# Low halves of the weights: from a VectorE subtraction to a ScalarE negation and an accumulating DMA, with five raw buffers

## The chip, the core and the metric

One core of a Trainium2 chip runs the whole program in one launch. The metric is the device time of one execution in microseconds (us). The engines are TensorE (PE, with its weight loads listed apart as PEld), VectorE (DVE), ScalarE (ACT), GpSimd (POOL) and SyncE (SP), which only issues transfers here.

## What is computed

Two layers of an encoder over 512 tokens of width 1024, all in float32. Each layer has a modulated norm, one input projection into three token mixers (a convolution module, windowed attention, a two-way recurrence), an output projection, a second modulated norm and a gated feed-forward block with a width-3 convolution. The modulation vectors come from the conditioning vector `c` through `w_ada`.

```python
for l in range(DEPTH):                                   # DEPTH = 2
    mod = cond @ w_ada[l] + b_ada[l]                     # 6 x 1024 values per layer
    sh1, sc1, g1, sh2, sc2, g2 = jnp.split(mod, N_MOD, axis=-1)
    h = _rmsnorm(x, norm1_w[l]) * (1.0 + sc1) + sh1
    x = x + g1 * _token_mixers(h, w_in[l], ..., w_out[l])  # 1024 -> 3584 -> mixers -> 1024
    h = _rmsnorm(x, norm2_w[l]) * (1.0 + sc2) + sh2
    x = x + g2 * _conv_ffn(h, w_up[l], conv_f_w[l], w_down[l])   # 1024 -> 2 x 2816 -> 1024
return _rmsnorm(x, final_norm_w)
```

## The kernel before

Activations lie with channels on the 128 partitions and the 512 tokens along the free dimension. A matrix product in near-float32 precision is made from three products of `fp32r` halves: a weight `w` is split into `hi`, the value rounded to `fp32r`, and `lo = w - hi`; an activation likewise. `block` issues, for each 128x128 block of weights, `hi*hi`, `hi*lo` and `lo*hi` into the same PSUM tile.

The weights come as a list of chunks, in the order in which they are used: 128x1024 floats (512 KB) for a column of `w_in` or `w_up`, 128x512 for `w_out1`, 128x640 or 128x512 for `w_down1`, 128x768 for the first group of each stage. Three threads of the program carry them:

- `loader` (L351) takes a free raw buffer `wr` (three of them) and has SP load the next chunk into it.
- `splitter` (L358) takes a loaded chunk at most three ahead of the one in use (five for a "wide" chunk, which may also use idle buffers of other tags). It writes `hi` into a buffer `wh` on ACT or DVE, whichever the planner expects to be done first (`copy`, L396), then `lo` into a buffer `wl` on DVE (L368), and gives the raw buffer back. There are four `wh` and four `wl`.
- `next_chunks` (L372) and `tile_gemm` (L712) use them: one tile of 128 output channels at a time, 24 matmuls for a chunk of 8 blocks, 15 for one of 5, 12 for one of 4.

All program order is fixed beforehand. `Clock` books an estimated end for each instruction, and `run_threads` always advances the thread of highest priority whose needs are met by that clock. Every engine, and SP's list of loads, then runs its instructions strictly in the order so written; an instruction that waits holds all behind it on its engine.

Three more threads matter here. `ada_thread` (L524) loads the rows of `w_ada`, 512 KB at a time, into buffers named `bias` and `wa` (three in the feed-forward stage), and has DVE reduce each with one 128x1024 instruction (`ada_tile`). Most of this work for layer 1 is put into the feed-forward stage of layer 0. `ffn_col` (L1304) takes an up-projection tile out of PSUM: one ACT and two DVE operations for the convolution, a GELU on ACT for the gate, a multiplication on DVE, and a split into halves `m` (copy and subtraction). `down` (L1295) runs the down-projection of a group of five or four columns once all its `m` are there; it is placed behind the first column of the next group.

The order of a layer is: mixers (`w_in` tiles with the mixers' small products between them, then `w_out`), then the feed-forward stage (a first group of six tiles, then up tiles and `down` groups by turns, then a last group that also feeds the next norm).

Of the kernel before, what the change touches and what calls it, by code (L numbers as in the profile page):

```python
# [9 lines left out]
F32 = mybir.dt.float32  # L10
F32R = mybir.dt.float32r
U8 = mybir.dt.uint8
AF = mybir.ActivationFunctionType
ALU = mybir.AluOpType
# [6 lines left out]
KD = D // 128  # L21
# [17 lines left out]
H2 = T // 2  # L39


BUFFERS = dict(wr=(4, 3), wh=(4, 4), wl=(4, 4), hx=(4, 8), qk=(4, 2), PT=(4, 4), KK=(4, 1), QQ=(4, 1), S=(4, 1),
               TT=(6, 1), ao=(2, 2), vr=(2, 2), va=(2, 1), bias=(4, 2), wa=(4, 1), tmp=(2, 5), P=(2, 2), sc=(1, 1),
               ap=(4.25, 1), acc=(2, 2), sm=(0.03125, 8), km=(2, 1), gs=(2, 3), qr=(2, 2), t2=(2, 2))
ORDER = ["wh", "wl", "wa", "bias", "wr", "tmp", "km", "P", "ap", "acc", "gs", "qr", "vr", "va", "ao", "t2", "sc",
# [16 lines left out]
def size(ap):  # L62
    n = 1
    for d in ap.shape[1:]:
        n *= d
    return n


def span(ap):
    lo = hi = ap.offset  # L70
    for s, n in ap.ap[1:]:
        if s > 0:
            hi += s * (n - 1)
        else:
            lo += s * (n - 1)
    return lo, hi
# [21 lines left out]
DM = 1.0  # L98
# [94 lines left out]
class Kernel:  # L193
    def __init__(self, ctx, tc, a):
# [13 lines left out]
        self.free_slots, self.slot, self.count = {}, {}, 0  # L208
        for tag, (kb, n) in BUFFERS.items():
            self.free_slots[tag] = [dict(tag=tag, name=f"{tag}{i}", size=int(kb * 256), pool=self.one, last=0.0)  # L210
# [51 lines left out]
    def dma(self, out, in_, eng=None):  # L262
# [7 lines left out]
            c.w.setdefault(out.tensor.name, []).append((lo, hi, t + (4.5 if eng is self.nc.gpsimd else 2.4), "DMA"))  # L270
        c.last[sb.tensor.name] = t + 2.0

    def mm(self, out, lhsT, rhs, start, stop, **kw):
        self.nc.tensor.matmul(out, lhsT=lhsT, rhs=rhs, start=start, stop=stop, **kw)  # L274
        n, m = size(out), out.shape[0]
        c = 0.009 + n * 0.000408 if rhs.dtype == F32R else n * 0.00168 * {32: 0.5, 64: 0.51}.get(m, 1.0)
        self.clk.issue("PE", c, [out], [lhsT, rhs])
# [80 lines left out]
    def splitter(self):  # L358
        for i in range(len(self.chunks)):
            more = MTAG + ["bias", "wa", "ap"] if i in self.wide else []  # L360
            yield (lambda: 0.0 if i in self.raw and i <= self.cur_chunk + (WA if i in self.wide else 3) else None,)
            t = self.raw.pop(i)
            yield (t, [["wh"] + more, 1], [["wl"] + more, 1])
            hi = self.sb([128, 1024], ["wh"] + more, F32R)[:, :t.shape[1]]
            self.copy(hi, t)
            yield (hi, DM, [["wl"] + more, 1])
            lo = self.sb([128, 1024], ["wl"] + more, F32R)[:, :t.shape[1]]
            self.v.tensor_tensor(out=lo, in0=t, in1=hi.bitcast(F32), op=ALU.subtract)  # L368
            self.give(t)
            self.wt[i] = (hi, lo)  # L370

# [671 lines left out]
    def rec(self, l, p):  # L1043
# [13 lines left out]
        def scores(lhs, rhs, w):  # L1057

            ps = self.pst("m2", [128, 2, 512])
            for c in range(4):  # L1060
                for hd in range(2):
                    for j in range(4):
                        mm(ps[32 * j:32 * j + 32, hd, c * w:(c + 1) * w], lhs(hd, c * 128 + 32 * j),
                           rhs(hd, c * 128 + 32 * j), True, True, tile_position=(64 * hd, 32 * j))
            return ps[:, :, :4 * w].rearrange("p h (c w) -> p h c w", c=4)
# [75 lines left out]
        for d in range(2):  # L1141
            cs = range(3) if d == 0 else range(1, 4)
            kt = kts[d]
            yield (kt, "m")
            u = self.pst("m", [128, 4, 128])
            for c in cs:
                mm(u[:, c], kt[:, c], V[:, c], True, True)
            self.give(kt)
            yield (u,)
            st = self.st[d]  # L1150
            seq = list(cs) if d == 0 else list(cs)[::-1]
            for i, c in enumerate(seq):
                for hd in range(2):
                    r = slice(64 * hd, 64 * hd + 64)
                    if i == 0:
                        v.tensor_copy(st[r, i, r], u[r, c, r])
                    else:
                        v.scalar_tensor_tensor(st[r, i, r], st[r, i - 1, r], TT[r, d, 128 * c:128 * c + 1], u[r, c, r],
                                               ALU.mult, ALU.add)
            self.give(u)  # L1160
# [3 lines left out]
        for c in range(4):  # L1164
            for hd in range(2):
                mm(o[:, c, 64 * hd:64 * hd + 64], S[:, hd, c], V[:, c, 64 * hd:64 * hd + 64],
                   c == 0 and hd == 0, False)
            last = [x for x in ((1, c - 1) if c > 0 else None, (0, 2 - c) if c < 3 else None) if x]
            for i, (qi, si) in enumerate(last):
                mm(o[:, c], QQ[:, qi, c * 128:(c + 1) * 128], self.st[1 - qi][:, si],  # L1170
                   False, c == 3 and i == len(last) - 1)
# [265 lines left out]
```

## Time and profile before

| | |
|---|---|
| median of three runs | 1370.12 us (1370.08 to 1370.56) |
| the profiled execution | 1370.76 us, span 1369.0 us |
| mean granted TensorE clock | 0.991 |
| PE busy | 1344.9 us (98%) |
| DVE busy | 1070.0 us (78%) |
| ACT busy | 609.6 us (45%) |
| POOL busy | 2.1 us |
| transfers | 169.19 MB, 37.9% of the 16 DMA engines' time on SP's queue |

By the tiles that the rows name, the mixers of layer 0 run until about 317 us of the span, the feed-forward stage of layer 0 from there to about 705 us, the mixers of layer 1 to about 972 us, and its feed-forward stage to the end. A "window" row gives, for a stretch of the span, its length, each engine's busy time with the number of instructions, the granted clock, the mean busy share of the DMA engines and the rate of transfer. A "group" row gives instructions of one kind and shape: count, busy time, mean ns of one, and the idle time before them with what ended it.

### The profile page before, as it was taken

The page shows a single profiled execution, that of the slowest core. Times are in us where ns is not written, and L with a number is a line of the kernel's source. Part 1 is how long each engine was busy: PE and PEld are TensorE (multiplying, and loading weights), DVE is VectorE, ACT ScalarE, POOL GpSimd, SP SyncE. Part 2 cuts the span into 40 slices and gives each one's busy share as a digit, 9 for nine tenths or more (in the row PEclk, how much of TensorE's full clock was granted, in tenths as well). Part 3 has the DMA queues.
Part 4 walks back from the last instruction along what each step waited for, and adds up shares of the span by engine and source line. Part 5 has one row for each costly group of instructions (what it writes and reads, how often), then busy time and mean ns, then how long its engine had stood idle before and what let it go on. Part 6 is the DMA issues. An engine that isn't in the chain of part 4 may idle for free.

```text
span 1369.0 us, 24502 instructions
## 1 busy us (share of the span) xinstructions
PE 1344.9 (98%) x10042; PEld 1112.4 (81%) x10042; DVE 1070.0 (78%) x1841; ACT 609.6 (45%) x1017; POOL 2.1 (0%) x16
## 2 busy tenths in 40 slices
PE   8999999999999999999999999999999999999997
PEld 7977767778988888888899777777898888888887
DVE  6799999898599999766695999888868565556666
ACT  4537556565342433333453473746535232233332
POOL 0000000000000000000000000000000000000000
PEclk8999999999999999999999999999999999999998
DMA  9534443232348788432431312011422323323221
GB/s 353 189 134 142 124 151 94 81 105 89 103 148 293 254 280 290 126 108 70 140 99 63 106 54 99 32 53 54 139 78 57 128 76 95 101 86 122 77 93 63
DMA packets 55264, 169.19 MB, mean 124 GB/s; under 512 B 6256, under 2 KB 8304, under 8 KB 55152
## 3 DMA queue, kind: packets, MB, share of 16 engines
q1 hardware_dynamic: 55152, 167.63, 37.9%
q8 instruction: 79, 1.29, 0.4%
q14 instruction: 33, 0.27, 0.1%
HBM read 165.50 MB, written 2.10 MB: 122 GB/s over the span
## 4 chain that ended last, share of the span: by engine, by line
PE 84%; DVE 12%; ACT 2%; issue 1%; DMA 0%; SPq 0%; DVEq 0%; ACTq 0%
PE m L274 53%; PE g L274 29%; DVE acc L181 2%; PE m L280 2%; DVE KK L181 2%; DVE QQ L181 1%; DVE wl L181 1%; DVE TT L181 1%; DVE wa L181 1%; DVE P L181 1%; DVE hx L181 1%; DVE x L181 1%; DVE st L181 0%; DVE sc L181 0%; DMA x<-xT 0%
## 5 line engine op out<-in xcount | busy, mean ns | idle before, releaser
L274 PE MATMUL g<-hx,wh 128*128 128x512 f32 (+1 forms) x1288 | 402.6, 390 | 0.9 <-DVE qk L181 0.8
L274 PE MATMUL m<-hx,wh 128*128 128x512 f32 (+1 forms) x1136 | 318.0, 364 | 0.0
L181 DVE TENSOR_TENSOR wl<-wr,wh 128x1024 fp32r<-128x1024 f32 (+3 forms) x215 | 220.5, 1027 | 90.4 <-ACT wh L181 79.4
L274 PEld LDWEIGHTS g<-hx,wh 128*128 128x128 f32 x1288 | 237.2, 189 | 53.2 <-issue 7.7
L181 ACT CAST wh<-wr 128x1024 fp32r<-128x1024 f32 (+3 forms) x176 | 157.1, 893 | 250.9 <-PE m L274 155.0
L274 PE MATMUL g<-hx,wl 128*128 128x512 f32 (+1 forms) x648 | 252.7, 390 | 0.0
L274 PEld LDWEIGHTS m<-hx,wh 128*128 128x128 f32 x1136 | 204.3, 189 | 34.2 <-issue 0.6
L274 PE MATMUL m<-hx,wl 128*128 128x512 f32 (+1 forms) x576 | 209.0, 363 | 0.0
L274 PEld LDWEIGHTS g<-hx,wl 128*128 128x128 f32 x648 | 122.5, 189 | 25.4 <-issue 3.8
L274 PEld LDWEIGHTS m<-hx,wl 128*128 128x128 f32 x576 | 108.7, 189 | 16.9
L181 DVE SCALAR_TENSOR_TENSOR x<-m,mod,x 128x256 f32<-128x256 f32 (+1 forms) x112 | 66.2, 592 | 43.1 <-PE m L274 42.1
L181 DVE SCALAR_TENSOR_TENSOR acc<-ap,par,acc 128x512 f32<-128x512 f32 x120 | 89.8, 748 | 2.2
L181 DVE SCALAR_TENSOR_TENSOR tmp<-m,par,tmp 128x511 f32<-128x511 f32 x120 | 89.1, 746 | 1.9
L181 ACT ACTIVATE P<-P,sm 128x512 f32<-128x512 f32 x72 | 51.5, 721 | 42.6 <-DVE sm L181 42.2
L181 ACT ACT_TABLE_LOAD x49 | 62.9, 1283 | 6.0 <-DVE sm L181 4.5
L181 DVE CAST wh<-wr 128x1024 fp32r<-128x1024 f32 (+3 forms) x41 | 24.5, 598 | 52.4 <-PE m L274 37.1
L181 ACT ACTIVATE tmp<-tmp 128x512 f32<-128x512 f32 x44 | 27.8, 632 | 73.1 <-DVE tmp L181 73.0
L181 ACT COPY km<-KK 128x512 f32<-128x512 f32 x30 | 20.5, 683 | 80.2 <-DVE KK L181 58.8
L181 ACT ACTIVATE tmp<-m,par 128x512 f32<-128x512 f32 x60 | 40.7, 686 | 34.5 <-PE m L274 32.8
L181 DVE CUSTOM_DVE_ANT_0 bias<-bias,cb,par 128x1024 f32<-128x1024 f32 x39 | 49.5, 1278 | 2.3 <-DMA bias<-w_ada 2.3
L181 DVE CUSTOM_DVE_ANT_0 wa<-wa,cb,par 128x1024 f32<-128x1024 f32 x39 | 49.9, 1278 | 0.7 <-DMA wa<-w_ada 0.7
L181 ACT ACTIVATE tmp<-x 128x256 f32<-128x256 f32 (+1 forms) x64 | 28.4, 444 | 46.4 <-DVE x L181 42.4
(319 smaller groups left out, 2158.0 us busy)
## 6 DMA issues: line engine op xcount, KB each, us to landing
wr<-w_up SPq DMA_DIRECT2D x76, 512.0 KB, 3.5
wr<-w_in SPq DMA_DIRECT2D x44, 512.0 KB, 3.5
bias<-w_ada SPq DMA_DIRECT2D x39, 512.0 KB, 4.5
wa<-w_ada SPq DMA_DIRECT2D x39, 512.0 KB, 4.0
wr<-w_down SPq DMA_DIRECT2D x32, 320.0 KB, 2.9
wr<-w_down SPq DMA_DIRECT2D x32, 256.0 KB, 2.6
wr<-w_in SPq DMA_DIRECT2D x16, 384.0 KB, 4.4
wr<-w_up SPq DMA_DIRECT2D x16, 384.0 KB, 3.3
```

The source lines that it names most:

```text
L181: r = f(*a, **k)
L274: self.nc.tensor.matmul(out, lhsT=lhsT, rhs=rhs, start=start, stop=stop, **kw)
L280: self.nc.tensor.transpose(out, in_, self.ident)
```

## The change

For every chunk but the first eight of layer 0 (`i < KD`), the subtraction on DVE is taken out. ACT writes `-hi` into the `wl` buffer, and a DMA that GpSimd issues then adds the raw chunk to it in place (`accum_op=ALU.add`, from `wr` to `wl`, both on chip). The raw buffer is free once that transfer has landed, and the `lo*hi` matmul waits for it. The planner books such an add on a line of its own, beside that of the loads. There are five raw buffers in place of three; the room comes from a smaller scratch area for GpSimd's descriptors.

```diff
-BUFFERS = dict(wr=(4, 3), wh=(4, 4), wl=(4, 4), ...
+BUFFERS = dict(wr=(4, 5), wh=(4, 4), wl=(4, 4), ...
...
+    def add_dma(self, out, in_):
+        self.nc.gpsimd.dma_start(out=out.bitcast(F32), in_=in_, accum_op=ALU.add)
+        c = self.clk
+        t = max(c.t.get("ADD", 0.0), c.t["PE"], c.written(out) or 0.0) + size(in_) * in_.shape[0] * 4 / 200e3
+        c.t["ADD"] = t
+        lo, hi = span(out)
+        l = c.w.setdefault(out.tensor.name, [])
+        l[:] = [e for e in l if not (lo <= e[0] and e[1] <= hi)] + [(lo, hi, t + 2.4, "DMA")]
+        c.last[in_.tensor.name] = c.last[out.tensor.name] = t + 2.4
...
             hi = self.sb([128, 1024], ["wh"] + more, F32R)[:, :t.shape[1]]
             self.copy(hi, t)
-            yield (hi, DM, [["wl"] + more, 1])
             lo = self.sb([128, 1024], ["wl"] + more, F32R)[:, :t.shape[1]]
-            self.v.tensor_tensor(out=lo, in0=t, in1=hi.bitcast(F32), op=ALU.subtract)
+            yield (hi, DM) if i < KD else (hi,)
+            if i < KD:
+                self.v.tensor_tensor(out=lo, in0=t, in1=hi.bitcast(F32), op=ALU.subtract)
+            else:
+                self.s.activation(lo, hi.bitcast(F32), AF.Copy, scale=-1.0)
+                yield (lo,)
+                self.add_dma(lo, t)
             self.give(t)
...
-    nc = bacc.Bacc("TRN2", target_bir_lowering=False, num_devices=1)
+    nc = bacc.Bacc("TRN2", target_bir_lowering=False, num_devices=1, dynamic_dma_scratch_size=4096)
```

Counted in the written order, 240 chunks change: 136 of 128x1024, 48 of 128x512, 32 of 128x640 and 24 of 128x768, 103.8 MB in all. Since the planner's clock for DVE changes, the whole order is written anew. Two places show what that does.

The first is SP's list of loads in the feed-forward stage of layer 0, before and then with the change. `wr<-w_down` is a chunk of weights; `wa<-w_ada` and `bias<-w_ada` are rows of the modulation matrix of layer 1.

```order
L263 DMA wr_781_5136<-w_down 128x640
L263 DMA bias_782_5144<-w_ada 128x1024
L263 DMA wr_788_5173<-w_down 128x640
L263 DMA wa_789_5185<-w_ada 128x1024
L263 DMA bias_793_5199<-w_ada 128x1024
L263 DMA wr_795_5217<-w_down 128x640
L263 DMA bias_796_5226<-w_ada 128x1024
L263 DMA wr_802_5252<-w_down 128x640
L263 DMA wa_803_5266<-w_ada 128x1024
L263 DMA bias_804_5274<-w_ada 128x1024
```

Here one or two modulation loads stand between two chunks of weights.

```order
L263 DMA wr_780_5170<-w_down 128x640
L263 DMA wa_781_5173<-w_ada 128x1024
L263 DMA bias_782_5183<-w_ada 128x1024
L263 DMA bias_783_5193<-w_ada 128x1024
L263 DMA wr_788_5212<-w_down 128x640
L263 DMA wa_789_5221<-w_ada 128x1024
L263 DMA bias_791_5234<-w_ada 128x1024
L263 DMA bias_796_5255<-w_ada 128x1024
L263 DMA wr_797_5264<-w_down 128x640
L263 DMA wa_798_5276<-w_ada 128x1024
```

With the change three stand there. The second place is DVE in the same stretch. `ISA` with a `wa` or `bias` operand is the reduction of one modulation load, `SCALAR_TENSOR_TENSOR tmp` the two convolution steps of an up tile, `TENSOR_TENSOR wl` the subtraction for `lo`.

```order
L181 TENSOR_TENSOR wl_801_5242<-wr_781_5136,wh_798_5234 128x640
L181 SCALAR_TENSOR_TENSOR tmp_800_5238<-m_0_791_5193,par,tmp_800_5238 128x511 x2
L181 TENSOR_TENSOR PT_797_5230<-tmp_792_5195,PT_797_5230 128x512
L181 ISA wa_789_5185,mod_157<-wa_789_5185,cb,par 128x1024
L181 ISA mod_157 128x1
L181 ISA bias_793_5199,mod_157<-bias_793_5199,cb,par 128x1024
L181 ISA mod_157 128x1
L181 TENSOR_TENSOR wl_808_5286<-wr_788_5173,wh_805_5278 128x640
L181 SCALAR_TENSOR_TENSOR tmp_807_5282<-m_799_5236,par,tmp_807_5282 128x511 x2
```

Between the convolution steps of two tiles DVE has a subtraction and two reductions.

```order
L181 SCALAR_TENSOR_TENSOR tmp_795_5245<-m_786_5198,par,tmp_795_5245 128x511 x2
L181 ISA wa_789_5221,mod_159<-wa_789_5221,cb,par 128x1024
L181 ISA mod_159 128x1
L181 SCALAR_TENSOR_TENSOR amul_161<-mod_159,par 128x1
L181 ISA bias_791_5234,mod_159<-bias_791_5234,cb,par 128x1024
L181 ISA mod_159 128x1
L181 ISA bias_796_5255,mod_159<-bias_796_5255,cb,par 128x1024
L181 ISA mod_159 128x1
L181 SCALAR_TENSOR_TENSOR amul_161<-mod_159,par 128x1
L181 SCALAR_TENSOR_TENSOR tmp_803_5293<-m_794_5243,par,tmp_803_5293 128x511 x2
```

With the change the subtraction is gone and a third reduction stands in its place. On ACT each `CAST wh` is now followed, one or two instructions later, by an `ACTIVATE wl<-wh` of the same width. TensorE's order has the same instructions, with the mixers' small products placed anew among the `w_in` tiles.

More of the change, by code (lines that the diff above doesn't have):

```diff
@@ L39 @@
 H2 = T // 2
-BUFFERS = dict(wr=(4, 3), wh=(4, 4), wl=(4, 4), hx=(4, 8), qk=(4, 2), PT=(4, 4), KK=(4, 1), QQ=(4, 1), S=(4, 1),
+BUFFERS = dict(wr=(4, 5), wh=(4, 4), wl=(4, 4), hx=(4, 8), qk=(4, 2), PT=(4, 4), KK=(4, 1), QQ=(4, 1), S=(4, 1),
                TT=(6, 1), ao=(2, 2), vr=(2, 2), va=(2, 1), bias=(4, 2), wa=(4, 1), tmp=(2, 5), P=(2, 2), sc=(1, 1),
```

## The prediction

> **What bounds the kernel now.** I read the page's busy shares first, then windows by stage, then the groups of the instructions that change, then the transfers.
>
> ```profile
> PE 1344.9 (98%) x10042; PEld 1112.4 (81%) x10042; DVE 1070.0 (78%) x1841; ACT 609.6 (45%) x1017; POOL 2.1 (0%) x16
> ```
>
> The page gives shares over the whole span; the windows say where PE is not full. Columns: stretch, its length, PE, PEld, DVE, ACT, POOL busy, granted clock, DMA share, GB/s.
>
> ```profile
> 15.00:65.00 50.00, 49.06 (x450) 44.92 (x450) 40.77 (x91) 22.67 (x48) 0.18 (x2) 0.91 0.76 270
> 65.00:120.00 55.00, 54.09 (x743) 42.09 (x742) 53.66 (x92) 25.71 (x45) 0.00 (x0) 1.00 0.46 152
> 120.00:180.00 60.00, 58.13 (x530) 42.28 (x528) 54.96 (x105) 36.46 (x60) 0.00 (x0) 1.00 0.38 115
> 180.00:250.00 70.00, 69.73 (x716) 51.47 (x716) 63.29 (x128) 43.32 (x83) 0.00 (x0) 0.98 0.40 128
> 250.00:317.00 67.00, 62.52 (x669) 43.84 (x669) 57.89 (x118) 41.90 (x77) 0.00 (x0) 1.00 0.27 83
> 375.00:668.00 293.00, 293.00 (x1294) 242.34 (x1293) 244.02 (x359) 101.50 (x143) 0.00 (x0) 1.00 0.57 188
> 740.00:820.00 80.00, 80.00 (x872) 61.77 (x872) 76.04 (x146) 47.31 (x80) 0.00 (x0) 1.00 0.22 72
> 820.00:900.00 80.00, 79.81 (x862) 59.70 (x859) 71.11 (x130) 42.98 (x77) 0.00 (x0) 1.00 0.18 59
> 900.00:972.00 72.00, 70.74 (x824) 52.78 (x823) 60.35 (x124) 45.12 (x85) 0.00 (x0) 1.00 0.30 89
> ```
>
> PE bounds nearly all of it. In the feed-forward stretch (375 to 668) it is busy for every microsecond: 293.00 us over 1294 matmuls are 0.2264 us each, so an up tile of 24 takes 5.43 us, a chunk of five blocks 3.40, one of four 2.72. In the mixers DVE is 90 to 98% busy, but PE idles only 0.91 + 1.87 + 0.27 + 4.48 = 7.5 us in layer 0 and 0.19 + 1.26 = 1.5 us in layer 1. Freeing DVE can win at most these 9.0 us, since the matmuls themselves stay.
>
> **The change, part by part.** Groups: busy, mean ns | idle before.
>
> ```profile
> L181 DVE TENSOR_TENSOR wl<-wr,wh 128x1024 fp32r<-128x1024 f32 x123 | 150.2, 1222 | 74.4 <-ACT wh L181 64.6 <-PE m L274 6.0 <-PE m L280 0.3
> L181 DVE TENSOR_TENSOR wl<-wr,wh 128x512 fp32r<-128x512 f32 x48 | 32.9, 686 | 8.9 <-ACT wh L181 8.0
> L181 DVE TENSOR_TENSOR wl<-wr,wh 128x640 fp32r<-128x640 f32 x32 | 26.1, 819 | 6.5 <-ACT wh L181 6.2
> L181 DVE TENSOR_TENSOR wl<-wr,wh 128x768 fp32r<-128x768 f32 x12 | 11.4, 952 | 0.7 <-ACT wh L181 0.6
> L181 ACT CAST wh<-wr 128x1024 fp32r<-128x1024 f32 x100 | 105.0, 1050 | 146.6 <-PE m L274 96.1 <-PE g L274 36.6 <-DMA wr<-w_up 9.2
> L181 ACT CAST wh<-wr 128x512 fp32r<-128x512 f32 x38 | 23.6, 621 | 42.6 <-PE g L274 21.3 <-PE m L274 21.1
> ```
>
> *Subtractions off DVE.* 136 x 1.222 + 48 x 0.686 + 32 x 0.819 + 24 x 0.952 = 248 us of DVE go. DVE is on PE's path only in the mixers; of the 9.0 us I take 2 as won, since 22 subtractions of 1.22 us in each layer's `w_in` tiles are some 27 us of about 230, an eighth of DVE's load, and part of the idle time is released by ACT. Ends: 0 and -9.
>
> *Negations on ACT.* A pass of the same width over on-chip data is nearest to the CAST rows: 1.05 us for 1024, 0.62 for 512. 240 of them make about 216 us, and ACT rises from 45% to some 60%. Taken at nothing: in the feed-forward stretch ACT is busy 101.5 of 293 us. If that cover went, `hi` of later chunks would be late, which the chain below prices.
>
> *Five raw buffers.* At the start two more chunks of 384 KB are loaded ahead of the modulation rows, with the DMA engines full. That is 0.79 MB at about 410 GB/s, 1.9 us; PE idles 0.94 us of 50 there, so little absorbs it, but these rows also have slack in their buffers. I take +1, ends 0 and +2. Elsewhere SP has more lead, which costs nothing.
>
> *The adds.* No row shows a transfer from GpSimd or between on-chip buffers. Two things must be priced: how late one lands, and how much of the DMA engines it takes. First the lateness, bounded by loads (size, us from issue to landing):
>
> ```profile
> wr<-w_up SPq DMA_DIRECT2D x76, 512.0 KB, 3.5
> wr<-w_down SPq DMA_DIRECT2D x32, 256.0 KB, 2.6
> PT<-w_sh SPq DMA_DIRECT2D x5, 512.0 KB, 8.2
> ```
>
> The chain for a chunk becomes cast, negation, add. Three chunks are split ahead: 16.3 us for up tiles, 8.2 us for four-block chunks. At the quiet end it takes 2 x 0.62 + 2.6 = 3.8 us for 256 KB and 2 x 1.05 + 3.5 = 5.6 for 512 KB; with the 8.2 us of a load into full queues, 9.4 and 10.3. I take the quiet end, since outside the start and the burst below the queues are less than half busy: covered, at nothing.
>
> Now the load on the DMA engines. This is the stretch that decides, the burst of modulation loads in layer 0's feed-forward stage, beside the start of the program, where the engines run full:
>
> ```profile
> 10.00:15.00 5.00, 4.81 (x27) 4.71 (x28) 2.09 (x4) 2.95 (x5) 0.00 (x0) 0.50 1.03 417
> 20.00:25.00 5.00, 5.00 (x41) 4.39 (x40) 4.86 (x10) 1.70 (x5) 0.00 (x0) 0.64 1.04 408
> 411.00:445.00 34.00, 34.00 (x151) 27.91 (x150) 30.97 (x49) 9.93 (x12) 0.00 (x0) 1.00 0.83 292
> 445.00:479.00 34.00, 34.00 (x152) 28.15 (x151) 32.72 (x50) 13.84 (x20) 0.00 (x0) 1.00 0.78 254
> 479.00:513.00 34.00, 34.00 (x152) 28.15 (x151) 33.29 (x55) 10.05 (x15) 0.00 (x0) 1.00 0.82 280
> 513.00:548.00 35.00, 35.00 (x156) 29.00 (x155) 33.08 (x49) 12.36 (x17) 0.00 (x0) 1.00 0.83 287
> ```
>
> The same stretch, DVE's reductions and what DVE waited for (us in total, times, longest):
>
> ```profile
> L181 DVE CUSTOM_DVE_ANT_0 bias<-bias,cb,par 128x1024 f32<-128x1024 f32 x31 | 39.4, 1278 | 2.3 <-DMA bias<-w_ada 2.3
> L181 DVE CUSTOM_DVE_ANT_0 wa<-wa,cb,par 128x1024 f32<-128x1024 f32 x16 | 20.4, 1278 | 0.5 <-DMA wa<-w_ada 0.5
> DVE bias L181 <- DMA bias<-w_ada: 2.3, 2, 1.4
> DVE wa L181 <- DMA wa<-w_ada: 0.5, 1, 0.5
> ```
>
> Before, DVE paces the burst (33 of 34 us busy) and the DMA engines are 80% busy, so DVE loses only 2.8 us to late loads. With the subtraction gone the written order fills DVE with reductions. Laying PE's order out at 0.2264 us a matmul, the 102 us from the first `down` on hold 45 modulation loads where they held 32. That is 45 x 0.524 = 23.6 MB, and the weights bring 65.5 KB per 0.679 us, 9.8 MB: 33.4 MB, 328 GB/s, before a single add. The adds carry another 9.8 MB.
>
> At the 410 GB/s of the full engines the loads take 81.5 us and the adds 23.9 us times a factor k. A load reads a byte once and writes it once. An add reads two operands and writes one, so k lies between 1 and 2, and I take 1.5 by that count of passes. Together that is 105, 117 or 129 us for k = 1, 1.5, 2 against 102 us of PE work: late by 3, 15 or 27 us. At the poorer rate of the burst itself (0.83 busy at 290, so 350 GB/s when full) and k = 2 it is 151 us, late by 49.
>
> Late loads hold DVE, which is in order, and behind the reductions stand the convolution steps. What lies between them and PE:
>
> ```profile
> L181 ACT ACTIVATE tmp<-m,par 128x512 f32<-128x512 f32 x60 | 40.7, 686 | 34.5 <-PE m L274 32.8 <-DVE KK L181 1.1 <-DVE tmp L181 0.6
> L181 DVE SCALAR_TENSOR_TENSOR tmp<-m,par,tmp 128x511 f32<-128x511 f32 x120 | 89.1, 746 | 1.9
> L181 DVE TENSOR_TENSOR tmp<-tmp,tmp 128x512 f32<-128x512 f32 x48 | 32.9, 689 | 4.5 <-ACT tmp L181 3.6
> L181 ACT CAST PT<-tmp 128x512 fp32r<-128x512 f32 x16 | 9.9, 620 | 42.7 <-DVE tmp L181 42.7
> L181 DVE TENSOR_TENSOR PT<-tmp,PT 128x512 fp32r<-128x512 f32 x16 | 11.0, 691 | 8.2 <-ACT PT L181 8.2
> ```
>
> A group's last column needs 0.69 + 2 x 0.75 + 0.69 + 0.62 + 0.69 = 4.2 us after its tile, and `down` starts two up tiles, 10.9 us, later: 6.7 us of slack. ACT's GELU waits for the same DVE steps, and the casts and negations stand behind it. So PE loses the lateness less 6.7 us: 8 us for k = 1.5, none for k = 1, 20 for k = 2, 42 at the worst end.
>
> A rule of the Trainium skill speaks against that cost. "DMA: Bandwidth & Descriptors", section "Anatomy of one DMA — SWDGE (gpsimd) path", fits a transfer from GpSimd as about 2.0 us plus its bytes at 436 GB/s; by it the adds would weigh like copies, the burst would hold, and the sum would end at the second rival below. No run here shows it for an add.
>
> **The sum:** -2 + 0 + 1 + 0 + 8 = +7 us on the profiled execution's 1370.76 us (0.6 us above the median of the runs): 1377 after rounding down the tenths.
>
> **The rivals.**
>
> *Adds too slow one by one* (slower). With the landing of the 8.2 us row the chain for 256 KB is 9.4 us, above the lead of 8.2 us, the point from which it decides. With four `wl` buffers a chunk then takes a quarter of chain plus use. At 12 us that is (12 + 2.72) / 4 = 3.68 us for 2.72, and 48 chunks of that width lose 46 us: about 1416. For it: nothing shows how fast GpSimd issues. Against it: a chain above 8.2 us needs a landing three times the quiet one. The Trainium skill's "SBUF — State Buffer", section "Who interferes with whom", says that DVE copies and casts in a two-port mode lock GpSimd out while they run, and descriptors wait; it adds to this chance, and no run here shows it.
>
> *Adds like copies* (faster). With k = 1 the burst is late by 3 us, less than the slack; the start costs nothing, and the mixers keep 3 to 9 of their idle us: 1361 to 1367, say 1365. For it: DVE's 90 to 98% in the mixers. Against it: the burst has 3 us of margin over a fully loaded DMA.
>
> *Nothing to win* (same). The burst holds, and the new order of the mixers' small products idles PE as much as the old one: 1369 to 1372.
>
> **How the numbers follow.** A difference of 0.2%, 2.7 us, is about what a measurement of this kernel can tell from none. The crowded burst has 0.46 (0.43 slower, 0.03 within), slow adds 0.14 (slower), adds like copies 0.25 (0.22 faster, 0.03 within), nothing to win 0.15 (0.09 within, 0.03 on either side). Faster 0.25, same 0.15, slower 0.60. The likeliest case is 1377, its own range 1373 (the slack eats most) to 1410 (350 GB/s, k = 2). The range takes in adds like copies but for its best end and the crowded burst but for its worst: 1363 to 1406.
>
> **What would show it.** In the burst, DVE's waits for `bias` and `wa` loads rise from 2.8 us to over 15, the DMA share goes to about 1.0, and PE is no longer busy for all of the stretch. Over the span DVE falls to about 840 us and ACT rises to about 800; PE's idle time in the mixers stays within 9 us. If the burst's waits stay at a few us, the price of an add (k) was too high; if PE waits for DMA into `wl`, the add's landing was underestimated. A time above 1410 or below 1361 makes the prediction wrong altogether.

## The result, and the profile after

| | before | with the change |
|---|---|---|
| median | 1370.15 us (1370.08 to 1370.56) | 1444.35 us (1440.78 to 1446.29) |
| the profiled execution | 1370.76 us, span 1369.0 us | 1440.78 us, span 1439.0 us |
| mean granted clock | 0.991 | 0.980 |

The medians are of four runs each (for before, the three of the table ahead and one of 1370.19 us). The ratio is 1.0538 (interval 1.0515 to 1.0561): the change costs 74 us. The prediction had the sign (slower, 1377 us) and a tenth of the size; 1444 us lies above its range and above the 1410 us that it called wrong altogether.

The page's first part, to be held against the row of before:

```profile
PE 1364.9 (95%) x10042; PEld 1126.1 (78%) x10042; DVE 874.8 (61%) x1648; ACT 771.4 (54%) x1205; POOL 210.9 (15%) x256
```

DVE lost the work it was to lose (195 us less: the 240 subtractions are gone, and some casts and copies came over from ACT) and ACT took the negations (162 us more: those into `wl` alone are 191, and 19 casts of weights moved to DVE). TensorE does the same 10,042 matmuls, yet idles 74 us of its span where it idled 24. The other 20 us of the 70 are in its busy time, 1364.9 us against 1344.9, at a lower mean clock (0.980 against 0.991). What is new is in the third part: queue, packets, MB, and the time of those packets as a share of 16 engines' span.

```profile
q0 software_dynamic: 34560, 103.82, 39.5%
q1 hardware_dynamic: 55152, 167.63, 34.1%
```

The adds (q0) carry 62% as many bytes as the loads and occupy the DMA engines longer. 103.82 MB in 0.395 x 1439.0 = 568 us are 183 GB/s; the loads run at 167.63 MB in 491 us, 342 GB/s. An added byte costs 1.87 loaded ones, or 2.24 at the 410 GB/s of full engines that the prediction used.

And in the sixth part: size, median us from issue to landing.

```profile
wl<-wr POOLq DMA_DIRECT2D x122, 512.0 KB, 6.2
wl<-wr POOLq DMA_DIRECT2D x48, 256.0 KB, 3.8
wr<-w_up SPq DMA_DIRECT2D x76, 512.0 KB, 5.8
bias<-w_ada SPq DMA_DIRECT2D x39, 512.0 KB, 7.7
```

An add of 512 KB lands 6.2 us after its issue where the prediction took 3.5, and the loads beside it became slower too (`w_up` 5.8 from 3.5, `bias` 7.7 from 4.5).

**Where the time went.** Both traces hold the same matmuls, and at the borders of stages in the same order. So the start of the n-th matmul in one trace less its start in the other tells how much had been lost by then, and differences of these give each stage its share. (Inside the mixers the small products stand in another order, so there only two kernels with the same order can be compared.) In us against the profiled execution of before, stages named by before's times; the experiments in the columns on the right follow below. The traced executions of the change, the copy and the spread are the shortest of their kernels, 4 to 8 us under the medians.

| stage | the change | no add | copy, not add | wide on DVE | spread | both |
|---|---|---|---|---|---|---|
| mixers of layer 0 with their last group, to 340 | +11.0 | -8.0 | -7.5 | +2.5 | +13.6 | +7.2 |
| the burst, 340 to 560 | +28.0 | -0.2 | +8.2 | +32.3 | +2.9 | +3.0 |
| rest of the up tiles, 560 to 668 | +0.2 | 0.0 | +0.6 | +5.0 | +2.3 | +2.5 |
| last group of that stage, to 736 | +11.5 | 0.0 | +2.8 | 0.0 | +12.8 | 0.0 |
| mixers of layer 1, to 971 | +4.3 | +4.0 | +4.0 | +4.0 | +4.1 | +4.8 |
| their last group, to 996 | +6.2 | 0.0 | 0.0 | 0.0 | +5.2 | 0.0 |
| feed-forward of layer 1, to 1324 | +0.2 | 0.0 | 0.0 | +2.0 | +1.1 | +1.6 |
| its last group and the end | +8.8 | +0.1 | +1.4 | 0.0 | +8.0 | +0.5 |
| total | +70.2 | -4.1 | +9.5 | +45.7 | +50.0 | +19.6 |

Two places carry most of the 70: the burst (28) and the last groups (11.5 + 6.2 + 8.8, and of the first row the 8.5 that go when the wide chunks stay on DVE, together 35).

**The burst.** The windows that the prediction showed of before, now with the change (length, PE, PEld, DVE, ACT, POOL busy, granted clock, DMA share, GB/s):

```profile
411.00:445.00 34.00, 34.00 (x151) 28.00 (x150) 22.07 (x38) 15.72 (x21) 6.03 (x7) 1.00 1.02 294
445.00:479.00 34.00, 28.76 (x125) 22.81 (x123) 19.75 (x34) 10.89 (x14) 4.34 (x5) 1.00 1.04 337
479.00:513.00 34.00, 28.85 (x108) 23.11 (x109) 25.11 (x41) 14.95 (x22) 4.30 (x5) 0.85 1.02 306
513.00:548.00 35.00, 28.86 (x112) 22.69 (x111) 25.91 (x46) 14.46 (x21) 6.89 (x8) 0.90 1.03 320
440.00:560.00 120.00, 102.73 (x412) 81.60 (x412) 78.38 (x134) 46.36 (x60) 17.28 (x20) 0.93 1.03 321
```

The DMA engines are full throughout, DVE is no longer busy, and from the second row on PE runs 108 to 125 matmuls where it ran 152 to 156. In the 120 us of the last row PE idles 17.3 us. Its 412 matmuls are 93.3 us of work at the 0.2264 us of before and took 102.7, so the lower clock (0.93) cost another 9.4 us. The waits of that stretch that bear on it (us in total, times, longest):

```profile
POOL wl L275 <- ACT wl L181: 97.0, 19, 10.5
ACT wh L181 <- DMA wr<-w_up: 25.1, 7, 5.3
DVE bias L181 <- DMA bias<-w_ada: 25.0, 15, 3.2
DVE wa L181 <- DMA wa<-w_ada: 18.4, 9, 2.8
ACT PT L181 <- DVE tmp L181: 18.0, 3, 8.2
ACT tmp L181 <- DVE tmp L181: 16.0, 5, 8.2
...
PE m L285 <- DMA wl<-wr: 11.0, 4, 5.2
PE g L285 <- DMA wl<-wr: 3.5, 2, 2.0
```

DVE waits for the modulation rows (43 us), and ACT for the convolution steps that stand behind them on DVE, up to 8.2 us at a time. Before, from 411 to 548 us, the longest such wait was 3.3 us:

```profile
ACT tmp L181 <- DVE tmp L181: 16.7, 7, 3.3
```

PE waits in the end for `wl`, the add. What made the add late is seen in the way to the longest of these waits (start, us, what, and in brackets the idle time before and its releaser):

```profile
463.68 1.29 DVE L181 CUSTOM_DVE_ANT_0 bias<-bias,cb,par 128x1024 f32<-128x1024 f32 x1 [1.31 <-DMA bias<-w_ada]
...
467.45 1.29 DVE L181 CUSTOM_DVE_ANT_0 bias<-bias,cb,par 128x1024 f32<-128x1024 f32 x1 [2.48 <-DMA bias<-w_ada]
...
468.86 1.52 DVE L181 SCALAR_TENSOR_TENSOR tmp<-m,par,tmp 128x511 f32<-128x511 f32 x2
470.48 0.63 ACT L181 ACTIVATE tmp<-tmp 128x512 f32<-128x512 f32 x1 [8.23 <-DVE tmp L181]
471.01 1.03 ACT L181 CAST wh<-wr 128x1024 fp32r<-128x1024 f32 x1
...
473.88 0.87 POOL L275 DMA_DIRECT2D wl<-wr  x1 [10.45 <-ACT wl L181]
...
482.11 0.79 PE L285 MATMUL m<-hx,wl 128*128 128x512 f32 x1 [5.21 <-DMA wl<-wr]
```

Two reductions wait for their rows, the convolution steps come late, ACT's GELU waits 8.2 us for them, and the cast and the negation of a chunk of weights stand behind the GELU. The add, issued at 473.9, needs 8.2 us to land, and PE stands still for 5.2 us. The waits of 2.0 and 3.5 us at 503 and 531 us came the same way, behind ACT's waits of 8.2 and 5.9 us for DVE; with the first they are 10.7 of the 14.5 us that PE waits for `wl`. The shorter waits at 448 and 455 us (3.2 together) follow casts that waited 3.5 and 4.1 us for late loads of weights. Over the 20 adds of the stretch the landing took 5.6 to 9.8 us, median 8.6.

**The last groups.** At the end of a stage several wide chunks are wanted at once, and their `lo` lies in idle buffers of other tags. Of the transfers issued from 130 to 330 us, which ends with the last group of layer 0's mixers:

```profile
wl<-wr POOLq DMA_DIRECT2D x11, 512.0 KB, 5.9
...
TT<-wr POOLq DMA_DIRECT2D x1, 512.0 KB, 9.4
S<-wr POOLq DMA_DIRECT2D x1, 512.0 KB, 10.8
qk<-wr POOLq DMA_DIRECT2D x1, 512.0 KB, 12.8
```

The adds into `TT`, `S` and `qk` were issued within 3 us of each other and landed one after another, after 9.4, 10.8 and 12.8 us. The end of layer 1's feed-forward stage shows what PE makes of it (start, us, and in brackets the idle time before and its releaser):

```profile
1399.14 0.39 PE L285 MATMUL m<-PT,ap 128*128 128x256 f32 x1 [1.87 <-DMA ap<-wr]
1399.37 0.39 PE L285 MATMUL m<-KK,S 128*128 128x256 f32 x2
1401.62 0.39 PE L285 MATMUL m<-KK,QQ 128*128 128x256 f32 x1 [1.86 <-DMA QQ<-wr]
1401.84 0.56 PE L285 MATMUL m<-TT,wh 128*128 128x256 f32 x2
1404.10 0.58 PE L285 MATMUL m<-TT,wl 128*128 128x256 f32 x1 [1.70 <-DMA wl<-wr]
```

### The profile page after: what moved, and what is told of

It is laid out like the page before. It is cut to its first block, busy times and chain, and to the rows that moved or that the text cites. A ratio compares the mean times of both kernels' runs of the same rounds, so it can differ in the third digit from the quotient of the medians.

```text
span 1439.0 us, 25211 instructions
## 1 busy us (share of the span) xinstructions
PE 1364.9 (95%) x10042; PEld 1126.1 (78%) x10042; DVE 874.8 (61%) x1648; ACT 771.4 (54%) x1205; POOL 210.9 (15%) x256
## 3 DMA queue, kind: packets, MB, share of 16 engines
q0 software_dynamic: 34560, 103.82, 39.5%
q1 hardware_dynamic: 55152, 167.63, 34.1%
## 4 chain that ended last, share of the span: by engine, by line
PE 64%; DMA 14%; issue 10%; DVE 8%; ACT 2%; POOL 1%; SPq 0%; POOLq 0%; DVEq 0%; ACTq 0%
PE m L285 39%; PE g L285 23%; DMA wl<-wr 3%; DMA bias<-w_ada 2%; DMA wa<-w_ada 2%; DMA qk<-wr 2%; DMA wr<-w_up 2%; DVE acc L181 1%; PE m L291 1%; DMA wr<-w_down 1%; DMA wa<-w_sh 1%; DVE st L181 1%; POOL wl L275 1%; DVE wa L181 1%; DVE tmp L181 1%
## 5 line engine op out<-in xcount | busy, mean ns | idle before, releaser
L285 PE MATMUL g<-hx,wh 128*128 128x512 f32 (+1 forms) x1304 | 408.7, 391 | 1.3 <-ACT tmp L181 1.3
L275 POOL DMA_DIRECT2D wl<-wr x213 | 185.1, 869 | 1125.1 <-ACT wl L181 958.0
L285 PE MATMUL m<-hx,wh 128*128 128x512 f32 (+1 forms) x1104 | 312.9, 368 | 0.0
L181 ACT CAST wh<-wr 128x1024 fp32r<-128x1024 f32 (+3 forms) x157 | 137.6, 876 | 171.0 <-PE m L285 73.4
L285 PEld LDWEIGHTS m<-hx,wh 128*128 128x128 f32 x1104 | 200.3, 190 | 34.0 <-issue 0.4
L285 PE MATMUL m<-hx,wl 128*128 128x512 f32 (+1 forms) x560 | 206.0, 368 | 8.7 <-DMA wl<-wr 8.7
L181 ACT ACTIVATE wl<-wh 128x1024 fp32r<-128x1024 f32 (+3 forms) x212 | 190.7, 900 | 43.0 <-DVE wh L181 39.1
L181 DVE CAST wh<-wr 128x1024 fp32r<-128x1024 f32 (+3 forms) x60 | 37.4, 623 | 141.2 <-PE m L285 113.6
L181 DVE SCALAR_TENSOR_TENSOR tmp<-g,par,tmp 128x511 f32<-128x511 f32 x56 | 41.8, 749 | 22.9 <-ACT tmp L181 21.9
```

The costliest lines, as they stand in the source:

```text
L181: r = f(*a, **k)
L275: self.nc.gpsimd.dma_start(out=out.bitcast(F32), in_=in_, accum_op=ALU.add)
```

## The experiments

The theory to be tested: an add is a dear transfer (about twice a load's time on the DMA engines, 6 us and more to land), and it costs at two places for two reasons, the burst by throughput and the last groups by latency. The rivals: that the change's other parts cost (five raw buffers, the negations on ACT, the new order), and that any transfer at that place, cheap or dear, would do the same. Each ratio below is against runs of before that were taken beside that kernel (medians 1370.7 to 1371.7 us).

**The wide chunks back on DVE.** The wide chunks (`self.wide`, at the ends and beginnings of the stages, 40 of the adds) are subtracted on DVE as before.

```diff
-            yield (hi, DM) if i < KD else (hi,)
-            if i < KD:
+            yield (hi, DM) if i < KD or i in self.wide else (hi,)
+            if i < KD or i in self.wide:
```

> Edit: the wide chunks (first and last groups of each stage) keep the subtraction on VectorE; all other chunks keep negation and add. Theory A (the last groups lose because their four 512 KB chunks are wanted almost at once and an add lands 6 to 12 us after issue, where the subtraction took 1.2 us): the 33 us lost at the four last groups go, the burst's 28 us stay, about 1411 us. Theory B (the adds lose only by filling the DMA engines): the last groups are not in the burst, so little changes, 1435 to 1444 us.

Measured: 1416.69 us (1410.86 to 1417.42), ratio 1.032 (1.0299 to 1.0341). In the table the last groups go to 0, and the burst stays (32.3). So the last groups' loss is the adds of their own chunks, in the first row too (8.5 us less).

**The modulation loads spread.** A distance of 5 us of TensorE's planned time between two reductions of `ada_thread` in the feed-forward stage.

```diff
-ADAG = 0.0
+ADAG = 5.0
```

> Edit: layer 1's modulation tiles are spaced at least 5 us apart by the planner (ADAG 0 to 5), so the loads of the feed-forward stage of layer 0 fall from 328 to about 200 GB/s. Theory A (burst: loads plus adds want more than the DMA engines give): the 28 us lost between the first and the second down-projection of layer 0 go, the last groups' loss stays, about 1416 us. Theory B (each add is late by itself, whatever the traffic): PE's waits for wl in that stretch stay, 1435 us or more.

Measured: 1425.22 us (1420.57 to 1426.82), ratio 1.0386 (1.0365 to 1.0406), 9 us above what was expected. The same stretch of the burst:

```profile
440.00:560.00 120.00, 117.91 (x517) 96.64 (x516) 66.45 (x106) 58.85 (x74) 22.41 (x26) 1.00 1.03 295
```

PE is busy for 117.9 of 120 us at full clock where it was busy for 102.7 at 0.93, and the loss falls from 28.0 to 2.9 us. The DMA engines still read 1.03, with fewer bytes a second: the modulation rows come later, and what is left still fills them. A share of 1 alone thus does not say that anything is late. What the stretch gained was partly given back: 2.6 us in the first row of the table, 2.1 from 560 to 668, 1.3 in the next last group.

**Both together.** The two edits above.

> Edits of the first two experiments together: wide chunks subtract on VectorE, modulation tiles spaced by 5 us. If burst and last groups are separate losses they add: about 33 and 24 us of the 70 go, and what stays is the mixers (3 to 8 us in layer 0, 4 in layer 1): 1380 to 1385 us. If one feeds the other, so that curing one cures part of the other, the sum would fall short: 1395 us or more.

Measured: 1389.54 us (1385.85 to 1391.99), ratio 1.0137 (1.0121 to 1.0153), a little above what was expected. The gains add, nearly: the last groups are at 0 as with the wide chunks alone, the burst at 3 as with the spread alone. What is left is 7.2 us in the mixers of layer 0 (4.7 more than with the wide chunks alone), 4.8 in those of layer 1, and 7.6 in small pieces of the feed-forward stages.

**A copy in place of the add.** The transfer goes between the same buffers but only copies; the low half then holds the raw weight, so this kernel computes something else.

```diff
-        self.nc.gpsimd.dma_start(out=out.bitcast(F32), in_=in_, accum_op=ALU.add)
+        self.nc.gpsimd.dma_start(out=out.bitcast(F32), in_=in_)
```

> Edit: the transfer that GpSimd issues copies the raw chunk over the buffer in place of adding to it (so the low half holds the raw weight); order, issue and bytes stay. If accumulating is what costs the DMA engines (two reads for one write), their time for the 103.8 MB falls from 39.5% of the span to about 22%, the burst's loss falls from 28 us to under 10, and the time to about 1410 us. If a transfer from GpSimd between on-chip buffers costs the same with and without the addition, the share and the time stay within 1% of 1444 us.

Measured: 1388.45 us (1380.3 to 1390.97), ratio 1.0113 (1.008 to 1.0146). Its queue, and its landings:

```profile
q0 software_dynamic: 27904, 103.82, 19.2%
```

```profile
wl<-wr POOLq DMA_DIRECT2D x122, 512.0 KB, 3.8
```

The same bytes at 103.82 MB / (0.192 x 1378.5 us) = 392 GB/s, 2.1 times the add's rate, and landed in 3.8 us where the add takes 6.2. With the same order of instructions as in the change, 56 of the 74 us go, and the time is 22 us below the 1410 us expected: the last groups gained too, which the expectation left out. So it is the accumulation, not a transfer at that place, that makes most of the loss. (The copies also went in fewer packets, 27,904 against 34,560; the next run holds the packets.) The burst still loses 8.2 us.

**Half an add.** Only the first half of each chunk's columns is added; the other half stays `-hi`.

```diff
-        self.nc.gpsimd.dma_start(out=out.bitcast(F32), in_=in_, accum_op=ALU.add)
+        n = size(in_) // 2
+        self.nc.gpsimd.dma_start(out=out.bitcast(F32)[:, :n], in_=in_[:, :n], accum_op=ALU.add)
```

> Edit: each add covers only the first half of the chunk's columns (the rest of the low half stays -hi); the order and the number of adds stay. If the loss is bytes through the DMA engines, the burst's 28 us fall to about 3 (loads 81.5 us and adds 22 us in 102 us of PE work) and the last groups' 33 us by a half: about 1400 us. If it is the fixed part of each transfer (issue, descriptors, landing), most of it stays: 1430 us or more.

Measured: 1394.11 us (1393.73 to 1396.42), ratio 1.017 (1.0153 to 1.0187). The sum is near what was expected, its parts are not: by the method of the table the burst loses 11.6 us where about 3 were expected, the mixers of layer 0 with their last group gain 4.5, and the other last groups lose 8.1, 0.0 and 2.9.

```profile
q0 software_dynamic: 34560, 51.92, 22.2%
...
wl<-wr POOLq DMA_DIRECT2D x122, 256.0 KB, 4.2
```

51.92 MB in 0.222 x 1392.0 = 309 us are 168 GB/s: the same number of packets with half the bytes takes 0.54 of the time, so the time goes with the bytes, nearly. Against the copy of the whole chunk (19.2%, 3.8 us) the half add is a little dearer in both, and the kernel with it a little slower: 1394 against 1388 us. The two make the transfers cheap in different ways, and the loss follows the time that they take.

**Only the buffers.** The kernel before with five raw buffers and the smaller scratch area, subtractions on DVE.

```diff
-BUFFERS = dict(wr=(4, 3), wh=(4, 4), wl=(4, 4), ...
+BUFFERS = dict(wr=(4, 5), wh=(4, 4), wl=(4, 4), ...
```

> Edit on the kernel before: five raw buffers and the small scratch, no adds, every subtraction on VectorE. If the buffers were a part of the loss or of a gain, the time would move by more than 0.2%. The theory that they are neutral (in the changed kernel the first 65 us are level with before): 1368 to 1373 us.

Measured: 1374.62 us (1373.64 to 1375.26), ratio 1.0029 (1.0017 to 1.004). Above the expected range: the buffers cost 3 to 4 us in this order, in the last stretch of layer 0's mixers (2.7 us from 310 to 317, 1.6 by 340), and none at the start, where the prediction had put its +1. The order of the mixers' small products changes with them, so buffers and order are not told apart; in the order of the change the same row is -8.0 without the add.

**Adds only in the mixers.** If freeing DVE pays anywhere, it is there. First chunks 14 to 29 alone (layer 0's `w_in` after the start), then 132 to 153 as well (layer 1's; the line that sets `add` then ends in `or 132 <= i < 154`).

```diff
-            yield (hi, DM) if i < KD else (hi,)
-            if i < KD:
+            add = 14 <= i < 30
+            yield (hi,) if add else (hi, DM)
+            if not add:
```

> Edit: adds only for 16 of the 22 w_in tiles of layer 0 (chunks 14 to 29), where VectorE is over 90% busy and the start's loads are over; all others subtract on VectorE. Theory: freeing VectorE there wins up to 8 us (the plain copy had the mixers of layer 0 shorter by 8), the adds' own traffic takes some back: 1362 to 1368 us. Rival: the win in the copy run came from traffic and not from VectorE, or the new order costs as much: 1369 us or more.

> Edit: as the run with adds in layer 0's mixers alone, and also for the 22 w_in tiles of layer 1. In layer 1 every variant so far lost 4 us in the mixers, whatever the transfers weighed, so the order or ScalarE is the cause there: 4 us above the run with layer 0 alone. If VectorE's relief wins in layer 1 as well, it is below that run.

Measured: 1376.58 us (1374.21 to 1378.83), ratio 1.0047 (1.0034 to 1.0061); and 1383.63 us (1382.88 to 1385.17), ratio 1.0098 (1.0084 to 1.0112). Both missed: no gain from the first, and 7 us lost by the second where 4 were expected. Against the kernel with five buffers alone the first is 2 us slower. Its loss is not the adds' alone: in the trace the mixers are 1.9 us behind before (2.9 with five buffers alone), and 2.3 us are lost in the burst, where it has no add and PE waits once, for 2.3 us, for a subtraction on DVE. In the second kernel the burst loses 4.5 us and the mixers of layer 1 3.9. Even where DVE is 90% busy the adds win at most that 1 us against the five buffers alone, in these orders.

**No add at all.** The negation and the written order stay, the transfer is left out, so the low half is `-hi` and this kernel, too, computes something else. It is what the change would give in this order if the add cost nothing, neither traffic nor a wait nor GpSimd's time.

```diff
-        self.nc.gpsimd.dma_start(out=out.bitcast(F32), in_=in_, accum_op=ALU.add)
```

> Edit: the add is left out altogether (the low half stays -hi); negations on ScalarE, buffers and planner's bookings stay. It is the ceiling of the change: VectorE relieved, no traffic added. If the adds' traffic is the whole loss, this run is level with the plain copy or below it: the mixers of layer 0 some 8 us shorter, those of layer 1 some 4 longer, burst and last groups at 0: 1362 to 1370 us. If ScalarE's negations or the new order of the burst and last groups cost by themselves, it stays above 1380 us.

Measured: 1367.39 us (1365.69 to 1370.65, 10 runs), ratio 0.9977 (0.9967 to 0.9986), within what was expected. The burst in it:

```profile
411.00:445.00 34.00, 34.00 (x151) 28.15 (x151) 25.67 (x44) 18.00 (x20) 0.00 (x0) 1.00 0.97 358
445.00:479.00 34.00, 34.00 (x151) 28.15 (x151) 32.64 (x57) 17.13 (x24) 0.00 (x0) 1.00 0.84 282
479.00:513.00 34.00, 34.00 (x151) 28.15 (x151) 26.11 (x44) 17.55 (x21) 0.00 (x0) 1.00 0.94 340
513.00:548.00 35.00, 35.00 (x156) 28.96 (x156) 15.79 (x23) 16.87 (x24) 0.00 (x0) 1.00 0.18 47
```

The crowded order of loads, by itself, costs nothing: PE is busy for every microsecond, and the DMA engines are done early (0.18 in the last row). So the adds' cost is the difference, 1444 - 1367 = 77 us, and the most that freeing DVE can bring in this order is about 3 us. The table says why so little: 8 us won in the mixers of layer 0 and 4.0 lost again in those of layer 1. The same 4 us stand in every column; whether the new order of the small products or ACT's negations cost them was not separated.

No kernel with the full computation came below before.

## Why the prediction was right in sign and wrong in size

*What is to be won: right.* PE's idle time in the mixers as the bound, 0 to -9, took -2. With the adds' cost taken out it is -4.1 in the trace and -3.3 in the medians.

*Negations hidden: right in effect.* ACT at 771 us (about 800 expected), DVE 875 (840). Without the add, ACT's extra 160 us cost nothing in the feed-forward stages (-0.2 to +0.1 in every such row).

*Five raw buffers, +1 (0 to +2): mis-sized.* 3.3 us in the trace of that kernel, at the end of the mixers and not at the start; in the order of the change no such loss shows.

*"Covered, at nothing": the step that failed first.* The add's landing was priced by a quiet load, 3.5 us for 512 KB. It is 6.2 in the median, 5.6 to 9.8 in the burst, up to 12.8 in the last groups. Up tiles outside the burst have 16.3 us of lead, and there the verdict held: 0.2 us in 330 us of layer 1's feed-forward stage. But the prediction looked at the steady stretches alone. In a last group the adds of several chunks are issued within some 10 us (three within 3 us at the end of layer 0's mixers) and all wanted within a few us of each other, so the lead of three chunks is no lead: 35 us. No term of the sum and no rival stood for them. The upper bound it wrote down, 8.2 us from the start of the program, was too low as well. Nor are the queues "less than half busy" outside the burst once the adds run in them: from 1100 to 1390 us the share is 0.81, though PE lost nothing there.

*The crowded burst, +8 for k = 1.5: the mechanism held, two terms were mis-sized.* Full DMA engines and waiting reductions came as announced (DVE's waits 43 us, over 15 expected; share 1.03). The path held too: late rows, late convolution steps, then the casts and negations that stand behind ACT's waits for those steps, as the prediction had said, and at its end the landing of the add, 8.6 us in place of 3.5. That is the sign it gave for a landing underestimated, PE waiting for a transfer into `wl`. A smaller part came over late loads of weights, which the prediction did not have.

The first wrong size is k. It is 1.87 against the loads' own rate and 2.24 against the 410 GB/s that the sum used, where "reads two operands and writes one" had been taken as 1.5, 2 at the most. With 2.24 the prediction's own sum is 81.5 + 9.8 x 2.24 / 0.410 = 135 us of transfers in 102 us of work, late by 33. The 43.2 MB of loads and adds at the 321 GB/s measured in the burst give 135 us as well. The second is the slack of 6.7 us, which is not to be seen in the cheaper transfers. By the same sum the copy is late by 4.5 us and the half add by 8.7, and their bursts lost 8.2 and 11.6: not less than the lateness, but more. So it is partly luck that 33 less 6.7, 26 us, comes near the 28 measured.

*Mixers.* PE's idle time was expected to stay within 9 us. Layer 0 went from -8.0 without adds to +11.0 with them, and copies in the same order keep -7.5, so it is again the add's price. Against the kernel without the add, which has the same order of matmuls, 8.5 of these 19 us are lost in the last group. Another 6.3 come from 65 to 125 us, where modulation rows and adds meet. The waits of DVE there, which before held none for a transfer:

```profile
DVE wa L181 <- DMA wa<-w_ada: 5.9, 3, 2.9
```

Most of the rest begins at 189 us, where PE waits 2.1 us for a load that ran beside adds and other loads:

```profile
PE m L285 <- DMA wa<-w_sh: 2.1, 1, 2.1
```

The clock then stands at 0.66 for the next ten microseconds. The prediction looked for adds and rows in each other's way in the burst alone.

*The rivals.* "Adds too slow one by one" had the right thing (late landings decide) at the wrong place: the four-block chunks on which it rested cost little, since a 256 KB add lands in 3.8 us. "Adds like copies" is the experiment with the copy, which even so was slower than before by 1.1%: at k = 1.05 (410 against 392 GB/s) the burst, late by 3 us in the rival's sum and covered by the slack, lost 8.2. The Trainium skill's fit for a transfer from GpSimd ("DMA: Bandwidth & Descriptors", "Anatomy of one DMA — SWDGE (gpsimd) path": about 2.0 us and the bytes at 436 GB/s, 3.2 us for 512 KB) is near the copy's 3.8 us and does not hold for an add's 6.2. The lock of GpSimd by DVE that the Trainium skill describes ("SBUF — State Buffer", "Who interferes with whom") left no mark to be told apart, and no run was made to separate it: GpSimd's idle time before the adds is put down to ACT (97.0 us in the burst).

## What to carry to other kernels

Price an accumulating transfer as its own kind, here about twice the engines' time of a copy and 6 us to land 512 KB, before it takes the place of a 1.2 us instruction on an engine that is not the bound. Ask of each transfer on the path not only whether the steady stretch covers it, but what happens where a stage ends and its last operands are wanted together. And run the ceiling, the change without its cost, early: one kernel said that in this order the idea could win no more than 0.23%.

## What the runs showed of the hardware

- An accumulating transfer between on-chip buffers ran at 183 GB/s (103.82 MB in 39.5% of 1439.0 us; 183 GB/s too with 86.00 MB in 33.9% of 1388.9), a plain copy of the same bytes at 392.
- An add kept GpSimd busy for 0.87 us in the mean, a copy of the same width for 0.54:

```profile
L275 POOL DMA_DIRECT2D wl<-wr x213 | 185.1, 869 | 1125.1 <-ACT wl L181 958.0
```

```profile
L275 POOL DMA_DIRECT2D wl<-wr x213 | 114.9, 539 | 1151.2 <-ACT wl L181 963.4 <-PE m L291 48.0 <-PE m L285 33.8
```

- After stalls of PE the granted clock fell to about half for some 7 us, so a wait costs more than its length. At the end of layer 1, where PE waits three times for 1.7 to 1.9 us:

```profile
1395.00:1401.40 6.40, 2.74 (x14) 1.95 (x12) 0.75 (x1) 3.59 (x4) 0.86 (x1) 1.00 1.02 201
1401.40:1408.80 7.40, 5.48 (x25) 5.19 (x26) 0.97 (x2) 0.83 (x2) 0.00 (x0) 0.54 0.23 44
1408.80:1416.00 7.20, 7.20 (x62) 7.20 (x62) 4.08 (x10) 1.91 (x5) 0.00 (x0) 1.00 0.00 0
```

PE ran 25 matmuls in 7.4 us (one wait of 1.7 us among them), then 62 in 7.2. The Trainium skill's "TensorE: Matmul & The Clock Gate", "Part 1: The HAM clock gate", puts the fall behind an idle window of about 3.4 us; here no single wait was that long, and two of 1.9 us, with three short matmuls between, were enough.
